# Branch B's query projected by features and read per group from scratch memory, in place of a token-major projection with transposes in attention

## The chip, the cores and the metric

The kernel runs on one NeuronCore of a Trainium2 chip. The metric is device time in microseconds (us) of one execution; the program is launched once and works through both layers. The engines are named as in the profile: PE (TensorE, with its weight loads as PEld), DVE (VectorE), ACT (ScalarE), POOL (GpSimd) and SP (SyncE, which here issues nearly all DMAs).

## The reference

Two layers of a hybrid decoder block over 512 tokens with 1024 features, all in float32. What matters here is branch B, a sliding-window attention with 16 query heads and 2 key/value heads of 64 features each:

```python
proj = h @ w_in                      # h = rmsnorm(x); all branches share one projection
# columns: DeltaNet q | k | v | z | beta | decay | SWA q (1024) | k (128) | v (128) | gates A, B
q = partial_rope(q_in.reshape(B, S, 16, 64), positions)   # rotates features 0..15 of each head
k = partial_rope(k_in.reshape(B, S, 2, 64), positions)
x1, x2 = xr[..., :8], xr[..., 8:]
rot = concatenate([x1 * cos - x2 * sin, x2 * cos + x1 * sin])
scores = einsum(q, k) * 64 ** -0.5   # 128 queries against the own and the previous 128 keys
p = softmax with a sink per head; o = p @ v
```

Branch A is a gated DeltaNet (short convolutions, decays, a chunked delta rule). Both branches are projected up, gated, merged, projected out, and followed by a feed-forward part with 4096 hidden features.

## The kernel before

**Numbers.** Every large product is made of three products in a reduced float32 type: each operand is split into a high part (a cast on ACT) and a remainder (a subtraction on DVE), and PE adds high x high, high x low and low x high in PSUM. Weights come as chunks of up to 128 x 1024 from one packed tensor; `load` (line 278) issues the DMA on SP, `prefetch` (376) makes the pair `wh`, `wl`. Six raw chunks (`WR`) and four pairs (`LOOK`) can be held ahead of use.

**Two ways to project.** `mm_a` (396) makes a feature-major tile: the weights stand still in PE and all 512 tokens move, 24 products of 512 columns to a PSUM tile of 128 features. `mm_a2` does it in two halves of 256 tokens. `mm_b` (415) and `mm_b4` (448) make token-major tiles: 128 tokens stand still and a strip of weight columns moves. Branch B's columns (beta, decay, q, k, v: 1296 in all) are projected token-major before, in three strips of `NB` = 432 columns, n = 0, 1, 2, each for four tiles of 128 tokens.

**Start of a layer.** The first strip is interleaved with the norm of the four token tiles. `turn` (542) transposes a normed tile on PE, `turned` (549) splits it into `hT`. In layer 0 this order is written out by hand for PE, ACT, DVE and SP (the `Order` object, 179, from line 610 to 677; `spin` fills PE with idle transposes). In layer 1 (681 to 691) only PE's order is written out, continuing that of the feed-forward tail. `rotary` (229) makes `cs`, the cosines and sines by token, once.

**Rest of B's projection.** Strips n = 1 and 2 (786) are projected into four PSUM tiles at a time, alternating between two sets (`four`, 492). `evac_b` (722) copies the strips into the token-major tiles `qt[t]` and `kv[t]`. In the middle of n = 1 stands `decays` (760): it cumulates DeltaNet's decays on PE, writes them to scratch memory, reads them back broadcast for each of 8 heads (`D`, 256 KB each), masks them on POOL, takes four exponentials a head on ACT (782) and writes them out again (`dd`).

**Attention beside other projections.** A loop over 16 groups (1044) runs one `att_group(t, g, e)` beside units of other projections: `MIX` lists them (G: merge gate B, K: DeltaNet key with convolution, A: gate A). A unit is one `mm_a`, 24 products of 512 columns, into the two-buffer PSUM pool `PM`. `att_rope(t)` (901) rotates all 16 query heads and 2 key heads on POOL, in tiles of 128 x 128. `att_prep` (918) splits v and transposes k. `att_q(t, g)` (941), called for every second group, transposes four 128 x 128 blocks of `qt[t]` on PE (945), scales, casts and splits them on ACT (950) and DVE (951) into the two tiles `qT` of 64 high rows and 64 low rows. `att_group` makes scores, masks, softmax on ACT and DVE, then transposes the probabilities (`ps_pt`, 1007) and multiplies them with v. The result replaces q in `qt[t]`.

**Order.** Outside the `Order` regions a planner places the instructions: it simulates the engines with costs of its own and picks, on each engine, the ready instruction that stands first in the program. On the chip each engine then runs its list strictly in that order. SP's list holds the weight loads and the scratch traffic together.

## Time and profile before

| | |
|---|---|
| median of 3 runs | 1817.72 us (1816.64 to 1817.88) |
| profiled execution, its own time | 1816.19 us |
| its span, first to last instruction | 1814.5 us |
| mean granted PE clock | 0.999 |
| busy: PE, DVE, ACT, POOL | 99%, 76%, 56%, 12% |
| HBM read, written | 239.38 MB, 37.36 MB |

PE's busy share includes modelled ends: a product is listed as busy until its result is drained, so consecutive products overlap in the list. What one product costs is the distance from its start to the next one's start. A row of the timeline gives start, duration, engine, line, operation, result and operands, and in brackets the engine's idle time ahead of it with what ended it.

### The profile page before, as it was taken

Reading aid. Unit: us, or ns where it says so; the run is one execution under the profiler, and the core shown is the slowest. Engines: PE = TensorE matmul, PEld = TensorE weight load, DVE = VectorE, ACT = ScalarE, POOL = GpSimd, SP = SyncE. Lnnn points to the kernel's source line nnn. Section 1 sums busy time; section 2 is a strip of 40 time slices with the busy share of each in tenths; the row PEclk is TensorE's granted clock in tenths of the full one; section 3 lists DMA queues with packets and bytes.
Section 4 is the critical chain, followed back from the end, with each engine's and each line's share of the span. In section 5 each row is a group of like instructions: output and inputs, shape, how many; then the busy total and the mean of one; then the engine's idle time right before and its main releaser. Section 6 shows DMA issues by size and latency. Waiting matters only on the chain.

```text
span 1814.5 us, 28394 instructions
## 1 busy us (share of the span) xinstructions
PE 1794.6 (99%) x10252; PEld 1524.7 (84%) x10252; DVE 1375.1 (76%) x2590; ACT 1007.5 (56%) x2065; POOL 210.6 (12%) x386
## 2 busy tenths in 40 slices
PE   9999999999999999999999999999999999999998
PEld 8878878888788888989898887888877888889896
DVE  5499796887666878898556997968875669698973
ACT  6678742444434656566556877234443347566572
POOL 0322102221101000000013221022111010000000
PEclk9999999999999999999999999999999999999999
DMA  5633447655463254554445334585545533555551
GB/s 201 203 112 121 111 146 226 178 172 152 117 208 129 82 164 156 174 180 145 168 160 176 106 127 111 169 232 159 163 140 154 171 116 105 174 162 164 174 178 56
DMA packets 146431, 278.60 MB, mean 154 GB/s; under 512 B 33569, under 2 KB 66657, under 8 KB 146290
## 3 DMA queue, kind: packets, MB, share of 16 engines
q1 hardware_dynamic: 145778, 276.75, 49.2%
q8 instruction: 81, 1.33, 0.3%
q14 instruction: 60, 0.49, 0.1%
q0 software_dynamic: 512, 0.03, 0.0%
HBM read 239.38 MB, written 37.36 MB: 153 GB/s over the span
## 4 chain that ended last, share of the span: by engine, by line
PE 88%; DVE 4%; ACT 4%; DMA 2%; issue 1%; POOL 0%; SPq 0%; DVEq 0%; POOLq 0%; ACTq 0%
PE ps_b L459 3%; PE ps_b L461 3%; PE ps_b L463 3%; PE ps_f L400 2%; PE ps_f L401 2%; PE ps_f L402 2%; PE ps_us L400 2%; PE ps_ud L400 2%; PE ps_us L401 2%; PE ps_ud L401 2%; PE ps_ud L402 2%; PE ps_us L402 2%; PE ps_vp L400 2%; PE ps_vp L402 2%; PE ps_vp L401 1%; PE ps_qp L401 1%
## 5 line engine op out<-in xcount | busy, mean ns | idle before, releaser
L384 ACT CAST wh<-wr 128x1024 fp32r<-128x1024 f32 (+2 forms) x368 | 372.7, 1019 | 430.4 <-PE ps_us L401 60.2
L385 DVE TENSOR_TENSOR wl<-wr,wh 128x1024 fp32r<-128x1024 f32 (+2 forms) x368 | 434.9, 1189 | 183.8 <-ACT wh L384 180.2
L526 POOL TENSOR_TENSOR pr<-pq,pw 128x1 f32<-128x1 f32 x16 | 9.8, 615 | 790.1 <-DVE pq L525 790.1
L459 PE MATMUL ps_b<-wh,h_h 128*128 128x432 f32 (+1 forms) x192 | 71.1, 370 | 0.0
L461 PE MATMUL ps_b<-wl,h_h 128*128 128x432 f32 (+1 forms) x192 | 70.4, 367 | 0.0
L463 PE MATMUL ps_b<-wh,h_l 128*128 128x432 f32 (+1 forms) x192 | 70.3, 366 | 0.0
L400 PE MATMUL ps_f<-g_h,wh 128*128 128x512 f32 x160 | 62.4, 390 | 0.0
L401 PE MATMUL ps_f<-g_l,wh 128*128 128x512 f32 x160 | 62.4, 390 | 0.0
L402 PE MATMUL ps_f<-g_h,wl 128*128 128x512 f32 x160 | 62.2, 389 | 0.0
L401 PE MATMUL ps_qp<-h_l,wh 128*128 128x512 f32 x128 | 53.9, 421 | 0.0
L400 PE MATMUL ps_vp<-h_h,wh 128*128 128x512 f32 x128 | 53.7, 420 | 0.0
L402 PE MATMUL ps_vp<-h_h,wl 128*128 128x512 f32 x128 | 53.7, 419 | 0.0
L995 ACT ACTIVATE M<-M,nm 128x128 f32<-128x128 f32 x128 | 49.8, 391 | 5.9 <-DVE nm L990 5.8
L400 PE MATMUL ps_qp<-h_h,wh 128*128 128x512 f32 x128 | 51.8, 405 | 0.0
L343 DVE TENSOR_TENSOR wr<-wr 128x512 f32<-128x512 f32 x72 | 47.5, 685 | 5.5 <-DMA wr<-in_weights_dram 5.2
L400 PE MATMUL ps_kp<-h_h,wh 128*128 128x512 f32 x128 | 51.6, 403 | 0.0
L402 PE MATMUL ps_qp<-h_h,wl 128*128 128x512 f32 x128 | 51.4, 401 | 0.0
L401 PE MATMUL ps_vp<-h_l,wh 128*128 128x512 f32 x128 | 51.3, 401 | 0.0
L401 PE MATMUL ps_ga<-h_l,wh 128*128 128x512 f32 x128 | 51.0, 398 | 0.0
L400 PE MATMUL ps_gb<-h_h,wh 128*128 128x512 f32 x128 | 51.0, 398 | 0.0
L402 PE MATMUL ps_kp<-h_h,wl 128*128 128x512 f32 x128 | 50.9, 398 | 0.0
L402 PE MATMUL ps_ga<-h_h,wl 128*128 128x512 f32 x128 | 50.7, 396 | 0.0
(435 smaller groups left out, 5928.4 us busy)
## 6 DMA issues: line engine op xcount, KB each, us to landing
wr<-in_weights_dram SPq DMA_DIRECT2D x320, 512.0 KB, 3.6
wr<-in_weights_dram SPq DMA_DIRECT2D x24, 432.0 KB, 5.2
D<-dd SPq DMA_DIRECT2D x32, 256.0 KB, 2.7
xd<-xo SPq DMA_DIRECT2D x12, 512.0 KB, 3.0
xt<-xd SPq DMA_DIRECT2D x24, 256.0 KB, 4.5
D<-gd SPq DMA_DIRECT2D x16, 256.0 KB, 6.2
dd<-D SPq DMA_DIRECT2D x16, 256.0 KB, 5.2
kkd<-kk SPq DMA_DIRECT2D x16, 256.0 KB, 2.0
```

The source lines that it names most:

```text
L343: tt(out=o_, in0=i0, in1=i1, op=ALU.add)
L384: nc.scalar.copy(wh[:, :w], wr[:, :w])
L385: sub(out=wl[:, :w], in0=wr[:, :w], in1=wh[:, :w].bitcast(F32), op=ALU.subtract)
L400: mm(ps, lhsT=wh[:, k, :], rhs=hi, start=k == 0, stop=False)
L401: mm(ps, lhsT=wh[:, k, :], rhs=lo, start=False, stop=False)
L402: mm(ps, lhsT=wl[:, k, :], rhs=hi, start=False, stop=k == KT - 1)
L459: mm(pss[t], lhsT=hi[:, tsl], rhs=wh[:, r, :], start=k == 0 and not onto, stop=False, skip_group_check=onto)
L461: mm(pss[t], lhsT=hi[:, tsl], rhs=wl[:, r, :], start=False, stop=False, skip_group_check=onto)
L463: mm(pss[t], lhsT=lo[:, tsl], rhs=wh[:, r, :], start=False, stop=k == KT - 1, skip_group_check=onto)
L526: ptt(out=r, in0=q1, in1=mhalf[:, 0:1], op=ALU.pow)
L995: act(out=M[:, j * P:(j + 1) * P], in_=M[:, j * P:(j + 1) * P], func=AF.Exp, bias=nm[:, j:j + 1], accum_out=den[:, j:j + 1])
```

## The change

Branch B's columns are split. Beta, decay, k and v (272 columns, `w_bkv`) stay token-major, now as the only strip; the weights come in three chunks with 2, 3 and 3 blocks of 128 rows (`BK`). q is projected feature-major in eight units like the other `mm_a` units. The host packs its columns so that feature d of all 16 heads lies together: unit u holds features 8u to 8u+7 of all heads, rows ordered (d, head). So units 0 and 1 hold the features that are rotated, and the rotation is six operations of DVE on whole 128 x 512 tiles, with cosines and sines turned to the same layout once (`turned_rotary`, layer 0; written to `csd` and read back in layer 1). Scaled high and low parts (`q_out`) are written to scratch memory `qd`; attention reads each group's `qT` from there by one DMA, issued one group ahead. `att_q`'s transposes, ACT and DVE work go, as do the copies into `qt` and the rotation of q on POOL. `decays` moves to the third q unit. In layer 1 the first q unit is put into the written-out order in two halves.

```diff
+    def turned_rotary(rot):
+        big = X4("cse")
+        b4 = big.rearrange("p (t s n) -> p t s n", t=NT, s=2)
+        for t in range(NT):
+            for s in range(2):
+                nc.gpsimd.tensor_copy(
+                    b4[:, t, s, :].rearrange("p (d h) -> p d h", d=HALF),
+                    cs[:, t, s, :].unsqueeze(2).broadcast_to([P, HALF, QH]))
+        for s in range(2):
+            ps = PS("ps_cs")
+            for t in range(NT):
+                tr(ps[:, t * P:(t + 1) * P], b4[:, t, s, :], ident)
+            nc.scalar.copy(rot[s], ps)
+            dma(csd[s], rot[s])
...
+    def mm_bkv(ps, ws, aT, t, ks=range(KT)):
+        tsl = slice(t * P, (t + 1) * P)
+        for k in ks:
+            hi, lo = aT[k]
+            j, = [i for i, (a, b) in enumerate(BK) if a <= k < b]
+            wh, wl = (w[:, k - BK[j][0], :] for w in ws[j])
+            mm(ps, lhsT=hi[:, tsl], rhs=wh, start=k == 0, stop=False)
+            mm(ps, lhsT=hi[:, tsl], rhs=wl, start=False, stop=False)
+            mm(ps, lhsT=lo[:, tsl], rhs=wh, start=False, stop=k == KT - 1)
...
-            for t in (None, 1, None, None, 2, None, 3):
+            for t in (None, 1, None, 2, None, 3):
...
-            for j in range(2):
-                part(0, j)
+            part(0, 0, 2)
             turned(ps0[1], 0, qs[1])
+            part(0, 2, 4)
             feed(2)
             q = sq(2)
             xs = [half(1, g) for g in range(2)]
-            part(0, 2)
+            part(0, 4, 5)
             ps1 = [turn(x_) for x_ in xs]
-            feed(3)
             rs.append(rstd("nr", *q))
-            part(0, 3)
+            part(0, 5, KT)
...
-            part(1, 0)
-            part(1, 1)
+            part(1, 0, 5)
             ps2 = [turn(x_) for x_ in xs]
             rs.append(rstd("nr", *q))
-            part(1, 2)
-            part(1, 3)
+            part(1, 5, KT)
...
-            part(0, 0, 6)
-            part(1, 0, 6)
-            part(0, 6, KT)
+            part(0, 0, 5)
+            part(1, 0, 5)
+            part(0, 5, KT)
+            part(1, 5, KT)
+            qf0 = PZ("ps_qf")
+            wq0 = weights()
+            mm_a2(qf0, hT, 0, wq0, range(0, 4))
             norm_turn(xs_next[2], 2, nxt[1])
-            part(1, 6, KT)
+            mm_a2(qf0, hT, 0, wq0, range(4, KT))
             norm_turn(xs_next[3], 3, nxt[1])
-            part(2, 0, KT)
-            part(3, 0, KT)
+            for a, b in ((0, 5), (5, KT)):
+                for t in (2, 3):
+                    part(t, a, b)
+            mm_a2(qf0, hT, 1, wq0)
...
         for t in range(NT):
-            evac_b(0, t, pb0[t])
+            nc.vector.tensor_copy(ba[:, t, :], pb0[t][:, 0:16])
+            nc.scalar.copy(kv[t][:, 0:256], pb0[t][:, 16:NB])
...
-        for n in range(1, 3):
-            pss = four(n)
-            mm_b4([p_[:, :NB] for p_ in pss], hT, decays if n == 1 else lambda: None)
-            for t in range(NT):
-                evac_b(n, t, pss[t])
+        rot = [T[2]("rot") for i in range(2)]
+        if l == 0:
+            turned_rotary(rot)
+        else:
+            for i in range(2):
+                dma(rot[i], csd[i])
+        qd8 = lambda i, u: qd[i, u * 8:(u + 1) * 8].rearrange("d h t -> (d h) t")
+
+        def q_out(u, src, scale=None):
+            hi, lo = pair(T[8], "qf")
+            if scale is None:
+                split(src, hi, lo)
+            else:
+                act(out=hi, in_=src, func=AF.Copy, scale=scale)
+                stt(out=lo, in0=src, scalar=scale, in1=hi.bitcast(F32), op0=ALU.mult,
+                    op1=ALU.subtract)
+            for i, a in enumerate((hi, lo)):
+                dma(qd8(i, u), a.bitcast(F32))
+
+        half_q = []
+        for u in range(NQU):
+            ps = qf0 if u == 0 else None
+            if ps is None:
+                ps = PM("ps_qf")
+                mm_a(ps, hT)
+            if u == 2:
+                decays()
+            if u >= 2:
+                q_out(u, ps, HD ** -0.5)
+                continue
+            a = T[1]("qa")
+            act(out=a, in_=ps, func=AF.Copy, scale=HD ** -0.5)
+            half_q.append(a)
+            if u == 1:
+                a, b = half_q
+                m = [T[3]("rm") for i in range(4)]
+                for i, (x_, r_) in enumerate(((a, 0), (b, 1), (b, 0), (a, 1))):
+                    tt(out=m[i], in0=x_, in1=rot[r_], op=ALU.mult)
+                tt(out=m[0], in0=m[0], in1=m[1], op=ALU.subtract)
+                q_out(0, m[0])
+                tt(out=m[2], in0=m[2], in1=m[3], op=ALU.add)
+                q_out(1, m[2])
...
-        def att_q(t, g):
-            ps = PS("ps_q")
-            for i in range(4):
-                j = g * 4 + i
-                tr(ps[:, i * P:(i + 1) * P], qt[t][:, j * P:(j + 1) * P], ident)
-            for e in range(2):
...
+        qgroups = qd[:, :, :, :].rearrange("a d (g j e) t -> (a d) g j e t", g=2, e=2)
+
+        def att_q(t, g, e):
+            a = T[7]("qT", F32R)
+            dma(c4(a.bitcast(F32)), qgroups[:, g, :, e, t * P:(t + 1) * P])
+            at["q", t, g, e] = a
...
+        att_q(*groups[0])
         for i in range(16):
+            if i < 15:
+                att_q(*groups[i + 1])
```

More of the change, by code (lines that the diff above doesn't have):

```diff
@@ L64, in chunk_order @@
         b_in = lambda w, r, c, n: out.append(("chunk", w, l, r, c, n))
-        for n in range(3):
-            for j in range(4):
-                b_in("w_in", j * 256, OFF_B + n * NB, NB)
+        for a, b in BK:
+            out.append(("chunk", "w_bkv", l, a * P, 0, (b - a) * NB))
+        for u in range(NQU):
+            a_in("w_q", u * 8)
         n_ = {"K": 0, "G": 0, "A": 0}
@@ L622, in hybrid_trunk @@
             sq = lambda t: (meansq(xts[t][:, :512], "nq0"), meansq(xts[t][:, 512:], "nq1"))
[L623 removed]
+            part = lambda t, a, b: mm_bkv(pb0[t][:, nbs], pre, hT, t, range(a, b))
             half = lambda t, g: norm_half(xts[t], gb, rs[t], g)
@@ L962, in att_group @@
                 att_rope(t + 1)
-            if e == 0:
-                att_q(t, g)
             w0 = max(t - 1, 0) * P
-            qh, den = at["q", e], sm.tile([P, 4], F32, name="den", bufs=4)
+            qh, den = at["q", t, g, e], sm.tile([P, 4], F32, name="den", bufs=4)
             kTh, kTl = kT[g]
```

86 lines of the change are left out of this document (43 added, 43 removed).

## The prediction

> **What bounds the kernel now.** I read the page first: shares of the engines and of the chain of waits.
>
> ```profile
> span 1814.5 us, 28394 instructions
> ...
> PE 1794.6 (99%) x10252; PEld 1524.7 (84%) x10252; DVE 1375.1 (76%) x2590; ACT 1007.5 (56%) x2065; POOL 210.6 (12%) x386
> ...
> PE 88%; DVE 4%; ACT 4%; DMA 2%; issue 1%; POOL 0%; SPq 0%; DVEq 0%; POOLq 0%; ACTq 0%
> ```
>
> PE sets the end nearly everywhere. So a step counts by the PE time it adds or removes, and by the PE waits it makes or ends. Second, the busy times by stage (span of the stage, then PE, PEld, DVE, ACT, POOL with counts, clock, DMA share, GB/s): layer 0's projection of B after its start, layer 0's attention, and the same two stages of layer 1.
>
> ```profile
> 33.00:71.00 38.00, 38.00 (x199) 36.61 (x198) 15.51 (x34) 27.43 (x69) 7.80 (x13) 1.00 0.75 243
> 71.00:245.00 174.00, 171.41 (x875) 138.97 (x874) 148.72 (x427) 131.86 (x386) 40.88 (x78) 1.00 0.37 113
> ...
> 930.00:968.00 38.00, 38.00 (x200) 36.65 (x199) 14.87 (x31) 25.95 (x66) 7.43 (x12) 1.00 0.75 241
> 968.00:1150.00 182.00, 178.61 (x907) 145.07 (x906) 154.89 (x441) 134.26 (x390) 44.16 (x80) 1.00 0.39 118
> ```
>
> In the projection stage PE has no gap, DVE is 40% busy and the DMA engines 75%. In attention PE idles 174 - 171.4 = 2.6 and 182 - 178.6 = 3.4 us, 6.0 in all, and DVE is 85% busy. These waits of PE, layer 0 then layer 1, say who is late there (times in total, count, longest):
>
> ```profile
> PE ps_pt L1007 <- ACT M L1001: 2.0, 3, 0.8
> ...
> PE ps_pt L1007 <- ACT M L1001: 1.9, 3, 0.7
> ```
>
> It is the softmax on ACT that PE's transposes of the probabilities wait for.
>
> **The change, part by part.** *The projection itself.* Third, the timeline of PE, for the distance of starts, 432 columns and 512 columns:
>
> ```profile
> 64.08 0.36 PE L459 MATMUL ps_b<-wh,h_h 128*128 128x432 f32 x1
> ...
> 64.66 0.36 PE L459 MATMUL ps_b<-wh,h_h 128*128 128x432 f32 x1
> ...
> 73.10 0.39 PE L400 MATMUL ps_gb<-h_h,wh 128*128 128x512 f32 x1
> ...
> 73.78 0.39 PE L400 MATMUL ps_gb<-h_h,wh 128*128 128x512 f32 x1
> ```
>
> Three steps lie between each two rows, so 0.193 us for 432 columns and 0.227 for 512: a fixed 0.013 plus 0.000417 a column, which gives 0.127 for 272 and 0.120 for 256. Before, a layer has 3 x 8 x 4 x 3 = 288 products of 432: 55.7 us. After, it has 96 of 272 (12.2) and 192 of 512 (43.5): 55.7 us. **0**. Splitting layer 1's first q unit in halves adds 24 products, 24 x 0.013 = **+0.3 us**.
>
> *The transposes in attention.* All 64 products of line 945, and one group of four with what follows it:
>
> ```profile
> L945 PE MATMUL ps_q<-ident,qt x64: 270/272/273, 76.6 to 1108.7; 128*128 128x128 f32 x64
> ...
> 76.61 0.60 PE L945 MATMUL ps_q<-ident,qt 128*128 128x128 f32 x4
> 76.97 0.47 PE L400 MATMUL ps_kp<-h_h,wh 128*128 128x512 f32 x1
> 77.28 0.39 PE L401 MATMUL ps_kp<-h_l,wh 128*128 128x512 f32 x1
> ```
>
> Four take 0.60 from first start to last end, so starts are (0.60 - 0.272) / 3 = 0.109 apart. The unit's product starts 0.36 after the first and takes 0.31 instead of 0.227 to the next: 0.36 + 0.08 = 0.44 for a group. There are 16 groups: **-7.0 us**, on the path, as PE's gaps there are 6.0 of 356 us. The turned cosines add 8 transposes in layer 0, 8 x 0.109 = **+0.9**.
>
> The Trainium skill ("TensorE: Matmul & The Clock Gate", Part 4, PE-mode transpose) gives about 275 ns for a transpose in a kernel's context; by it 56 fewer would be worth 15.4 us instead of 6.1. The row agrees as to duration, 272 ns, but the starts are 109 ns apart.
>
> *The start of layer 0.* Fewer columns per token tile leave PE less to do while the norms are made.
>
> ```profile
> 14.14 1.40 DVE L535 SCALAR_TENSOR_TENSOR xs<-x,nr,ps_row 128x512 f32<-128x512 f32 x2
> 15.37 1.04 PE L546 MATMUL ps_n<-ident,xs 128*128 128x128 f32 x8
> ...
> 16.62 1.29 DVE L552 TENSOR_TENSOR h_l<-ps_n,h_h 128x512 fp32r<-128x512 f32 x2
> ...
> 33.42 0.44 PE L459 MATMUL ps_b<-wh,h_h 128*128 128x432 f32 x1
> ```
>
> The second tile's transposes wait for its normed half; with a first weight chunk of 544 instead of 864 columns ahead of it I put them at 14.5 instead of 15.37. Behind them stand 81 products (10.3), three sets of eight transposes (2.4) and some 0.3 of waits: the stage ends near 27.5, 5.9 before 33.4. It hands 96 x 0.067 = 6.4 us of columns to the q units. Loss **+0.5**. A tile now costs PE 3.05 + 0.8 us against 1.29 + 1.40 on DVE plus ACT's cast, so DVE should keep up; ends: -0.5 (the smaller chunk lands sooner) and +2.0 (three tiles late by 0.5 each beside the 0.5).
>
> *What the q units add beside PE.* Per layer 8 casts and 2 copies on ACT replace 12 copies to `qt`, about even; DVE gets 8 splits and 6 rotation steps, 14 x 0.69 (the size of line 951, below) = 9.6 us in a stage where it idles 22. POOL makes 8 copies of 128 x 128:
>
> ```profile
> L912 POOL TENSOR_TENSOR rt<-qt,cs x8: 449/458/465, 69.3 to 1051.0; 128x128 f32<-128x128 f32 x8
> ...
> L951 DVE SCALAR_TENSOR_TENSOR qT<-ps_q,qT x32: 683/685/694, 79.0 to 1112.1; 64x512 fp32r<-64x512 f32 x32
> ...
> 32.87 0.32 ACT L256 ACTIVATE cs<-ang,hp 128x32 f32<-128x32 f32 x1
> ```
>
> 8 x 0.46 after 33.2 is 37, and rotation needs the tables at 27.5 + 0.9 + 2 x 5.44 = 39: hidden by the first two units, though by 2 us only. SP issues 16 writes and 16 reads more a layer, and two of the turned tables; weight loads stand behind the writes in its list, but run up to ten chunks (six raw, four split) ahead of use, 10 x 5.44 = 54 us: cost 0. The decays start at 27.5 + 0.9 + 16.3 = 44.7 in layer 0, and the first K unit, their first reader, ends at 27.5 + 0.9 + 43.5 + 10.9 = 82.8: cost 0. The writes are 4.2 MB in a stage that moves 243 GB/s at a share of 0.75: 13 us of full DMA time on 28.5, in 44 us. It fits, just; what is late first is the broadcast read of the decays.
>
> *The new wait there.* A q unit holds one of two PM buffers until ACT has cast it and DVE has split it, where four-tile sets had spare. And ACT has the decays. Layer 1, the decay product on PE and then ACT in order of time, with the copies of strip n = 1 among the exponentials:
>
> ```profile
> 940.34 0.30 PE L762 MATMUL ps_g<-lw,le 128*128 128x32 f32 x2
> ...
> 949.37 0.21 ACT L780 ACTIVATE egl<-D 128x4 f32<-128x4 f32 x1 [2.17 <-POOL D L778]
> ...
> 950.90 0.50 ACT L727 COPY qt<-ps_b 128x432 f32<-128x432 f32 x1
> ...
> 956.90 0.50 ACT L727 COPY qt<-ps_b 128x432 f32<-128x432 f32 x1
> ...
> 960.15 1.28 ACT L782 ACTIVATE D<-D,ngc 128x128 f32<-128x128 f32 x4
> ```
>
> From the decay product, exponentials fill ACT from +9.0 to +21.1, and copies got in at +10.6 and +16.6 only, because the decays stand first in the program. After, with zero at the end of unit u = 2, unit 4 ends at +10.9, its cast gets in at +16.6 and DVE frees the buffer at 16.6 + 0.6 + 0.7 + 0.1 = 18.0; PE has unit 5 until +16.3. Wait 1.6 a layer, **+3.2**. Ends: 0 (the cast gets in at once) and 22.5 - 16.3 = 6.2 a layer (it comes behind the last exponential), 12.4.
>
> *The trip through scratch memory.* The nearest row is the 256 KB round trip that the chain shows at the last head of DeltaNet, and PE's wait behind it:
>
> ```profile
> 462.10 3.77 DMA vxd<-kvx
> 466.02 3.40 DMA kvx<-vxd
> ...
> 469.95 0.49 PE L1264 MATMUL ps_y<-vs,Pt 128*128 128x128 f32 x2 [0.91 <-ACT vs L1247]
> ```
>
> From the end of unit 7 the first `qT` needs 0.6 + 0.7 + 7.2 = 8.5 us. PE has G and K units meanwhile, 2 x 5.44 = 10.9. If the planner puts the scores behind K, nothing is lost; right behind G, 3.1 a layer. I take 0.5, between no wait and the 0.9 of the row: **+1.0**, ends 0 and 6.2. Later groups are read a group ahead, over 8 us, and the DMA is at 0.37 there: 0. SP stands still while the first read waits for the last write; behind it are weights ten chunks ahead and K's scratch writes: 0.
>
> *What attention gets back.* ACT loses 2 x 0.59 and DVE 2 x 0.69 for each of 8 query blocks a layer, 9.4 and 11 us, and POOL's rotation goes. PE's 6.0 us of waits there are mostly behind ACT, so I take half, **-3.0**. Ends: -6.0 (all), and +2.0 (the order is planned anew, and one layer's waits for the softmax come twice).
>
> **Sum:** -7.0 + 0.9 + 0.3 + 0.5 + 3.2 + 1.0 - 3.0 = -4.1 us. The profiled execution, 1816.2 with a span of 1814.5, would take 1812.1; the median of the runs stands 1.5 higher, so I forecast 1817.7 - 4.1 = **1813.6 us**. All low ends give -12.3, all high ends +14.8.
>
> **Rivals.** *ACT holds the q units (slower).* The casts of units 4 and 5 come behind the last exponential in both layers, because D arrives later with the writes in the same DMA engines and ACT runs its list in order: +12.4 in place of +3.2, 1822.8. For it: ACT's solid 12 us, the DMA share of 0.75. Against: two copies did get in. It decides from a cast at +18.5 on: the wait is then 18.5 + 1.4 - 16.3 = 3.6 a layer, which with both layers eats the 4.1 saved; from +20.4 on the loss passes 0.2%.
>
> *Attention is filled by others (no change).* PE's order is planned around ACT and DVE; if the softmax stays as late as it is, half of the 7.0 turns into waits for it and none of the old waits goes: -4.1 + 3.5 + 3.0 = +2.4, 1820.1; with the casts in time as well, -0.8, 1816.9. For it: DVE at 85%; against: ACT and DVE lose more there than PE.
>
> *More than the sum.* No wait at the PM buffers or the first read and all 6.0 given back: -11.3, 1806.4. For it: attention's waits name ACT; against: the burst on ACT.
>
> *A transpose is worth its whole duration.* The 7.0 becomes 64 x 0.272 = 17.4 and the 0.9 becomes 2.2, so -4.1 - 10.4 + 1.3 = -13.2, 1804.5. For it: the mean duration in the row; against: the distances of starts, 0.109, which are what the next product waits for. The Trainium skill's price above ("TensorE: Matmul & The Clock Gate", Part 4) would come out here.
>
> **How the numbers follow.** About 0.2%, 3.6 us, is what a measurement of this kernel can tell from no change. Forecast 0.37, its own range 1809 to 1817; more than the sum 0.08; whole duration 0.02; attention filled 0.27; ACT holds 0.26. The forecast and the two larger gains make 0.47, of which the forecast's upper end passes 0.01 to no change: faster 0.46, same 0.27 + 0.01 = 0.28, slower 0.26. The range reaches from the larger gain to the slower rival: 1805.5 to 1824.
>
> **What would show it.** Line 945 gone, and products of 272 columns 0.127 apart (at 0.14, +1.2 a layer). The first product of the first q unit of layer 0 near 27.5. The gap ahead of q unit 6: 1.6, and 6 would be the slower rival. The first scores: no idle PE, or idle behind a DMA of `qd`. PE's wait for `M` halved in attention. If the projection stage has gaps at every unit, or weights are late, the sum is wrong in a part that I costed at nothing.

## The result, and the profile after

The changed kernel took 1826.87 us in the median of six runs (1825.28 to 1832.95), the kernel before 1817.8 in the same rounds. The ratio is 1.0057, with a 95% interval from 1.0043 to 1.0071: 0.57% slower, 9 us by the medians and 10 by the ratio, where the forecast was 4 us faster. It also lies above the range (1805.5 to 1824). The profiled execution took 1828.03 us, 1.2 above its median, as that of before lay 1.6 below its own; so the two traces differ by 11.85 us in span, 3 more than the medians.

The page of the changed kernel, its span, its busy times and its chain by engine:

```profile
span 1826.3 us, 28362 instructions
...
PE 1793.9 (98%) x10220; PEld 1508.5 (83%) x10220; DVE 1366.0 (75%) x2576; ACT 998.5 (55%) x2039; POOL 198.3 (11%) x346
...
PE 74%; DVE 7%; DMA 6%; ACT 6%; issue 4%; POOL 2%; SPq 1%; DVEq 0%; POOLq 0%; ACTq 0%
```

PE has 32 products fewer (64 transposes gone, 8 for the cosines and 24 halves added), as counted, and its busy time is lower. But PE held 88% of the chain before and holds 74% now: the time is not in products, it is in waits. PE's waits in the changed kernel (us in total, times, longest):

```profile
PE ps_y L1331 <- DVE rr L1328: 4.3, 6, 2.3
PE ps_s L1041 <- DMA qT<-qd: 2.8, 2, 1.9
PE ps_qf L435 <- DVE qf_l L838: 2.6, 2, 1.5
PE ps_pt L1071 <- ACT M L1065: 2.4, 3, 0.8
...
PE ps_o L1087 <- DVE pf_l L546: 2.0, 4, 1.5
PE ps_n L591 <- DVE xs L580: 1.7, 1, 1.7
PE ps_o L1087 <- POOL pc L1081: 1.6, 4, 0.6
```

In the kernel before, the wait for `rr` takes 1.2 us and the one for `pc` 0.6. The waits for `qT`, `qf_l`, `pf_l` and `xs` are not there, and the one for `M` is longer:

```profile
PE ps_pt L1007 <- ACT M L1001: 3.9, 6, 0.8
```

So PE waits 1.5 us less for the softmax (`M`), and 3.0 more for what is made of it, the split probabilities (`pf_l`) and the masked ones (`pc`). The timeline of PE in the changed kernel has, in layer 0 and in this order: the wait at the start, the first q unit, the wait ahead of q unit 6, the wait ahead of the first scores, and what follows them.

```profile
12.40 0.29 PE L458 MATMUL ps_b<-wh,h_l 128*128 128x272 f32 x1
14.40 1.38 PE L591 MATMUL ps_n<-ident,xs 128*128 128x128 f32 x8 [1.71 <-DVE xs L580]
...
26.80 0.29 PE L456 MATMUL ps_b<-wh,h_h 128*128 128x272 f32 x1
...
27.55 0.25 PE L743 MATMUL ps_cw<-ident,cwr 96*128 96x96 f32 x1
27.58 0.48 PE L435 MATMUL ps_qf<-h_h,wh 128*128 128x512 f32 x1
...
67.61 0.39 PE L437 MATMUL ps_qf<-h_h,wl 128*128 128x512 f32 x1
69.52 0.50 PE L435 MATMUL ps_qf<-h_h,wh 128*128 128x512 f32 x1 [1.53 <-DVE qf_l L838]
...
85.23 0.39 PE L437 MATMUL ps_kp<-h_h,wl 128*128 128x512 f32 x1
87.47 0.30 PE L1041 MATMUL ps_s<-kT_h,qT 128*128 128x128 f32 x1 [1.85 <-DMA qT<-qd]
...
89.38 0.42 PE L1041 MATMUL ps_s<-kT_h,qT 128*128 128x128 f32 x1
...
90.67 0.73 PE L435 MATMUL ps_kp<-h_h,wh 128*128 128x512 f32 x1
91.20 0.63 PE L436 MATMUL ps_kp<-h_l,wh 128*128 128x512 f32 x1
...
92.78 0.39 PE L437 MATMUL ps_kp<-h_h,wl 128*128 128x512 f32 x1
```

From 67.61 to 69.52 are 1.91 us where 0.227 is the distance of products: q unit 6 is 1.69 late. From 85.23 to 87.47 it is 2.01. And after that wait the products of 512 columns start 0.43 to 0.53 apart instead of 0.227. The windows of this stretch (length, PE, PEld, DVE, ACT and POOL busy, granted clock, DMA share, GB/s) show why:

```profile
84.00:88.00 4.00, 2.15 (x13) 1.56 (x12) 0.55 (x2) 0.26 (x1) 0.00 (x0) 1.00 1.02 275
88.00:90.00 2.00, 2.00 (x13) 1.87 (x13) 1.73 (x5) 0.85 (x1) 0.00 (x0) 0.80 0.60 220
90.00:92.00 2.00, 2.00 (x8) 1.77 (x8) 1.90 (x4) 1.98 (x11) 0.00 (x0) 0.50 1.01 317
```

The granted clock is 1.00 while PE idles, falls to 0.50 at 89.2, 1.7 us after the work has resumed, and is back at 1.00 from 92.6, 3.41 us later. From 89.38 to 92.78, six products of scores and five of 512 columns take 3.4 us in place of 6 x 0.111 + 5 x 0.227 = 1.8: the wait for q costs 1.6 us more than itself.

Where the 11.85 us lie, as distances between first starts in the two traces (first product of gate B, of the up-projection `ps_us`, of `ps_wo`, of layer 1's `ps_b`):

| stretch | before | after | difference |
|---|---|---|---|
| layer 0, start and B's projection | 71.04 | 75.11 | +4.07 |
| layer 0, attention | 175.26 | 177.27 | +2.01 |
| layer 0, from there to `ps_wo`, with the scan | 308.99 | 311.87 | +2.88 |
| layer 0, rest | 307.55 | 308.17 | +0.62 |
| layer 1, B's projection | 105.68 | 106.98 | +1.30 |
| layer 1, attention | 175.29 | 174.41 | -0.88 |
| layer 1, rest | 670.68 | 672.53 | +1.85 |

Attention, which was to give 10 us, gives nothing in the two layers together: 351.7 us here, 350.1 and 348.7 in two later runs with the same order of instructions, 350.6 and 350.3 in two profiles of the kernel before. The third row holds no edited line.

### The profile page after: what moved, and what is told of

Read it like the earlier page. It is cut to its first block, busy times and chain, and to the rows that moved or that the text cites. A ratio compares the mean times of both kernels' runs of the same rounds, so it can differ in the third digit from the quotient of the medians.

```text
span 1826.3 us, 28362 instructions
## 1 busy us (share of the span) xinstructions
PE 1793.9 (98%) x10220; PEld 1508.5 (83%) x10220; DVE 1366.0 (75%) x2576; ACT 998.5 (55%) x2039; POOL 198.3 (11%) x346
## 4 chain that ended last, share of the span: by engine, by line
PE 74%; DVE 7%; DMA 6%; ACT 6%; issue 4%; POOL 2%; SPq 1%; DVEq 0%; POOLq 0%; ACTq 0%
PE ps_f L435 2%; PE ps_f L436 2%; PE ps_f L437 2%; DMA fb<-fd 2%; PE ps_us L435 2%; PE ps_us L437 2%; PE ps_us L436 2%; PE ps_b L506 2%; PE ps_b L504 2%; PE ps_b L508 2%; PE ps_ud L436 2%; PE ps_ud L437 1%; PE ps_ud L435 1%; PE ps_qp L435 1%; PE ps_qp L436 1%
## 5 line engine op out<-in xcount | busy, mean ns | idle before, releaser
L436 PE MATMUL ps_kp<-h_l,wh 128*128 128x512 f32 x128 | 51.0, 399 | 0.0
L436 PE MATMUL ps_ud<-yT_l,wh 128*128 128x512 f32 x128 | 49.9, 390 | 0.8 <-DVE yT_l L546 0.8
L435 PE MATMUL ps_us<-oT_h,wh 128*128 128x512 f32 x128 | 50.0, 390 | 0.6 <-DVE qq L874 0.6
L435 PE MATMUL ps_ga<-h_h,wh 128*128 128x512 f32 x128 | 50.6, 395 | 0.0
L436 PE MATMUL ps_gb<-h_l,wh 128*128 128x512 f32 x128 | 50.5, 395 | 0.0
```

The costliest lines, as they stand in the source:

```text
L435: mm(ps, lhsT=wh[:, k, :], rhs=hi, start=k == 0, stop=False)
L436: mm(ps, lhsT=wh[:, k, :], rhs=lo, start=False, stop=False)
```

## The experiments

Each ratio is to the kernel before, in the same rounds.

**Attention alone, and the transposes put back.** The kernel before, with its own projection, but without transposes, splits and the 16-head rotation; q's own values are left out, `qT` comes from scratch memory filled once.

```diff
-            if e == 0:
-                att_q(t, g)              # 4 transposes, casts, splits
+            # all groups: qT by DMA from qd, one group ahead
+            dma(qrows[:, i * 2048:(i + 1) * 2048], a.bitcast(F32))   # qd filled once with hT
```

> The kernel before with the attention of the changed one alone: B's projection, its evacuations and q's strips stay; the 64 transposes, the splits behind them and the 16-head rotation are gone, and qT is read per group from scratch memory that was filled once, in layer 0, with the normalized activations' halves (4 transfers of 1 MB); q's own values are left out of the attention. The prediction's two gains (theory): 64 transposes at 0.109 us a start, 7.0 us, and 3.0 us that attention gets back: 1807.8 beside 1817.8. What the trace of the changed kernel shows behind its first scores (second theory): 0.66 us and 2.4 us shorter in the two layers, and 1.7 us more without the lowered clock: 4.8 us, so 1813.0. Filled by others (rival): the planner's products are spread over the same time and the waits for M and for the probabilities take the transposes' place: 1816 to 1818.

It took 0.9971 of the time before (0.9960 to 0.9983), 1813.31 us. That is 4 us gained by the medians and 5 by the ratio, about half of the 10. The second theory had the time, 1813.0, but from 0.7 and 2.4 us of attention and the clock; the stages give 1.8 and 1.9. Two of PE's waits have grown, from 3.9 us for `M` and 0.6 for `pc`:

```profile
PE ps_pt L1000 <- ACT M L994: 5.2, 6, 1.2
PE ps_o L1016 <- POOL pc L1010: 2.7, 4, 0.8
```

With the transposes gone PE idles for 9.1 us in the two attention stages where it idled for 6.3; nothing shows a gain from ACT's and DVE's lighter lists. To see which part gives the 4 us, the same kernel again with the 64 transposes put back into a buffer that nobody reads:

```diff
+            if e == 0:
+                ps = PS("ps_q")
+                for i in range(4):
+                    j = g * 4 + i
+                    tr(ps[:, i * P:(i + 1) * P], qt[t][:, j * P:(j + 1) * P], ident)
```

> The kernel before with the attention of the changed one, as before it (q read from scratch memory that was filled once; q's own values left out), but the 64 transposes of q are issued as in the kernel before, into a buffer that nobody reads; what stays away is their evacuation on ScalarE and VectorE and the rotation of 16 heads on GpSimd. Without them the kernel was at 0.9971 of the kernel before, 4.0 us less, and attention 1.8 us shorter in each layer. TensorE's count (theory): the 64 transposes start 0.091 us apart in the profile before, 5.8 us in all, and they come back in full where they are put back; the rest of attention gives 0 to 2 us: attention at 175 to 176 us again, the kernel at 1816 to 1819. Gaps (rival): the transposes lay in time in which PE waited for softmax anyway, and what was gained came from the evacuations: attention stays at 173.5 us and the kernel at 1813 to 1814.

It took 1.0014 (1.0006 to 1.0023), 1820.68 us: not the 0.9971 that the transposes in gaps would leave, but slower than before. The first products of gate B and of the up-projection bound the attention stage. Their groups (shortest, median and longest duration in ns, first and last start in us), layer 0 and layer 1, first of the kernel before:

```profile
L400 PE MATMUL ps_gb<-h_h,wh x64: 387/389/485, 71.0 to 218.8; 128*128 128x512 f32 x64
L400 PE MATMUL ps_us<-oT_h,wh x64: 389/389/468, 246.3 to 289.2; 128*128 128x512 f32 x64
...
L400 PE MATMUL ps_gb<-h_h,wh x64: 387/390/476, 968.5 to 1116.2; 128*128 128x512 f32 x64
L400 PE MATMUL ps_us<-oT_h,wh x64: 387/389/467, 1143.8 to 1186.8; 128*128 128x512 f32 x64
```

The same groups with the attention alone:

```profile
L401 PE MATMUL ps_gb<-h_h,wh x64: 387/390/481, 70.6 to 216.4; 128*128 128x512 f32 x64
L401 PE MATMUL ps_us<-oT_h,wh x64: 387/389/467, 244.1 to 287.1; 128*128 128x512 f32 x64
...
L401 PE MATMUL ps_gb<-h_h,wh x64: 387/389/480, 969.1 to 1114.9; 128*128 128x512 f32 x64
L401 PE MATMUL ps_us<-oT_h,wh x64: 389/389/472, 1142.5 to 1185.5; 128*128 128x512 f32 x64
```

And with the transposes put back:

```profile
L401 PE MATMUL ps_gb<-h_h,wh x64: 387/389/481, 70.4 to 219.3; 128*128 128x512 f32 x64
L401 PE MATMUL ps_us<-oT_h,wh x64: 389/389/470, 246.8 to 289.7; 128*128 128x512 f32 x64
...
L401 PE MATMUL ps_gb<-h_h,wh x64: 387/389/481, 969.4 to 1118.5; 128*128 128x512 f32 x64
L401 PE MATMUL ps_us<-oT_h,wh x64: 389/389/467, 1146.1 to 1189.1; 128*128 128x512 f32 x64
```

Attention takes 175.3 and 175.3 us before, 173.5 and 173.4 alone, 176.4 and 176.7 with the transposes. So putting 64 transposes back costs 2.9 + 3.3 = 6.2 us, 0.097 each (7 us by the medians of the whole kernel), and all else that attention is rid of (the evacuations and the rotation) is worth 1.1 + 1.4 = 2.5 us on the wrong side. PE idles for 7.7 us in these two stages, 1.4 more than before, so that much of the 2.5 is waiting. Freed time on ACT and DVE brought nothing here; the planner's new order is the likely reason of the 2.5, which no run shows.

**The projection alone.** The changed projection with its writes, and the attention of before on rows loaded from x in q's place.

```diff
+            dma(qt[t], x[t * P:(t + 1) * P, :])       # in place of q
-        att_q(*groups[0])                             # nothing read from qd
+            if e == 0:
+                att_q(t, g)                           # transposes as before
```

> The changed kernel's projection with the attention of the kernel before: q by features, rotated, split and written to scratch memory, but not read back; attention rotates 16 heads and transposes as before, on rows that are loaded from x in place of q (2 MB more to read in each layer). Additive (theory): what the projection adds in place by the trace, 4.1 us in layer 0 up to the first feature unit and 1.5 in layer 1, with nothing for the attention, 5.6 us over the kernel before: 1823.4. The prediction's own terms (0.3, 0.9, 0.5 and 3.2 us): 1822.7. The DeltaNet stages (rival): they are 2.9 and 1.4 us longer in the changed kernel with no edit in them; if the writes to scratch memory or the new buffers cause that, this kernel has it too, and comes to 1827; if it is not theirs, the stage from the first products of the scan to the up-projection takes what it takes in the kernel before, 188.6 us in layer 0.

1.0059 (1.0042 to 1.0076), 1827.8 us: 10 us, nearly twice the 5.6 of the theory. Its rival, which had the scan longer here too, had 1827. Attention takes 175.4 and 175.1 us in it, as before. In its trace the loss is 5.7 us by the first product of gate B in layer 0 (at 76.7), 5.6 in the scan of layer 0 and 4.9 in layer 1's projection, of which 2.0 are a wait of the transposes for a normed tile, with 3.41 us at half the clock behind it; the profiled execution, 1832.77 us, is 5 above the median, which is that much of this. The changed start is dearer than its first profile said: the first q unit, at 27.6 there, came at 27.5, 27.5, 29.3, 29.4, 29.7 and 30.0 in six other profiles with the same start. The granted clock parts them. In the last four it fell to 0.50 for 3.41 us at the wait for `xs` (1.72 to 1.81 us); in the other three (waits of 1.71, 1.26 and 1.08) it stayed at 1.00. From the transposes behind this wait to the first q unit are 14.4 to 14.7 us in the four and 13.1 to 13.2 in the three; the rest is that `xs` came 0.4 to 0.9 later. One window, first of the changed kernel's profile, then of a later run with the same order of instructions (the earlier evacuation, below) and a wait of 1.72:

```profile
16.00:18.00 2.00, 2.00 (x18) 2.00 (x17) 1.98 (x4) 2.00 (x6) 0.00 (x0) 1.00 0.90 291
...
16.00:18.00 2.00, 2.00 (x11) 2.00 (x10) 1.43 (x3) 1.57 (x5) 0.14 (x1) 0.50 0.94 371
```

**The q units: more buffers, or no burst ahead.** ACT's timeline of the changed kernel between units 2 and 7 (L837 is the cast of a unit, L820 the exponentials of the decays):

```profile
58.55 0.57 ACT L837 ACTIVATE qf_h<-ps_qf 128x512 fp32r<-128x512 f32 x1
59.02 2.44 ACT L820 ACTIVATE D<-D,ngc 128x128 f32<-128x128 f32 x8
...
62.44 3.61 ACT L820 ACTIVATE D<-D,ngc 128x128 f32<-128x128 f32 x12
...
68.17 0.57 ACT L837 ACTIVATE qf_h<-ps_qf 128x512 fp32r<-128x512 f32 x1
```

Between 59.1 and 68.2 no cast gets in, and unit 6 waits for the buffer. One variant gives it another buffer, one takes the burst away:

```diff
-                ps = PM("ps_qf")
+                ps = (PM, PM, PZ, PZ)[u % 4]("ps_qf")
```

> The changed kernel, but the q units go round four PSUM buffers (two of PM, two of PZ) where they had PM's two. The wait as a wait (theory): TensorE waits 1.69 us ahead of q unit 6 in layer 0 and 1.19 us in layer 1 only because both PM buffers are held until ScalarE's cast gets past the decay exponentials; with four buffers both go and the kernel is 2.9 us shorter than the changed kernel, 1824.0 beside 1826.9. The wait moves (rival): the casts still stand behind the exponentials, so the last units' halves are written as late as before, and the first read of q comes no earlier: the time lost ahead of unit 6 turns up ahead of the first scores (2.01 us there now, 3.7 or more then), and the kernel stays at 1826 to 1827.

```diff
             if u == 2:
-                decays()                    # all 8 heads' exponentials
+                dec = decays()              # yields behind each head
+                next(dec)
             if u >= 2:
                 q_out(u, ps, HD ** -0.5)
+                for _ in range((1, 2, 2, 2, 1, 0)[u - 2]):
+                    next(dec)
```

> The changed kernel, but the decay exponentials are not queued in one block behind q unit 2: one or two heads' stand behind each of units 2 to 6. Burst (theory): no cast of a q unit stands behind more than 3 us of exponentials, TensorE no longer waits ahead of unit 6 (1.1 to 1.7 us in layer 0 and 1.2 in layer 1 in the two profiles of this code), with two PM buffers as now, and the wait ahead of the first scores stays: 1824.0. Conserved (rival): as with four buffers, what is saved there is idle time ahead of the first scores, and the kernel stays at 1825.8 or above; a variant of the rival, exponentials now beside the last units' casts, would make that wait longer than 2.0 us.

With four buffers: 1.0041 (1.0026 to 1.0056), 1825.76 us, not told apart from the changed kernel. PE's rows of the first scores in it, layer 0 and layer 1:

```profile
86.57 0.30 PE L1041 MATMUL ps_s<-kT_h,qT 128*128 128x128 f32 x1 [2.84 <-DMA qT<-qd]
...
987.41 0.30 PE L1041 MATMUL ps_s<-kT_h,qT 128*128 128x128 f32 x1 [2.56 <-DMA qT<-qd]
```

The wait ahead of unit 6 is gone and the waits here have grown, 1.85 to 2.84 in layer 0. The buffers only passed the lateness on, as the rival had it. With the exponentials spread: 1.0012 (1.0002 to 1.0022), 1821.18 us, 6 us under the changed kernel by the medians and 8 by the ratios (4 by the ratio of the earlier evacuation, below, whose order of instructions is the changed kernel's), more than either theory gave: no wait ahead of any q unit (layer 1's projection 105.67 us, as before), idle 1.27 and 1.59 us ahead of the first scores, and no lowered clock anywhere in its profile. No other single edit gained as much. The two waits at the q units are 2.9 us of it; the first scores come no earlier than in the changed kernel (11.8 and 12.1 us behind gate B's first product), and what the rest is stays open.

**The first read.** One more unit ahead of the first scores, or the last unit's evacuation ahead of the next weights' cast:

```diff
-MIX = "G K K G K K G K K G K K G GA GA GA".split()
+MIX = "GK K G K K G K K G K K G GA GA G A".split()
```

> The changed kernel, but the first attention group has two feature units ahead of it (G and K) and every later unit goes one group earlier; the order of the units and their weights is the same, and the last group but one has one G less beside it. First read (theory): in layer 0 TensorE idles 2.01 us ahead of the first scores behind the transfer of qT from scratch memory and then runs 1.7 us late at a lowered granted clock, in layer 1 it idles 1.10; one more unit, 24 products of 0.227 us = 5.4 us, covers all of it, so the kernel is 4.8 us shorter than the changed kernel, 1822.1, with a granted clock of 1.00 throughout. Filler is only moved (rival): the unit now lacks at the end of the stage, where softmax sets the pace, and the wait comes back there as a wait of the transposes for M or of DeltaNet's first products; then 1826 to 1827 with no idle time ahead of the first scores.

```diff
-                mm_a(ps, hT)
+                mm_a(ps, hT, w=taken() if u == NQU - 1 else None)   # weights' next split behind q_out
```

> The changed kernel, but behind the last q unit its own evacuation (cast, subtraction, two writes) comes before the next weights' cast and subtraction, which stand ahead of it on ScalarE (1.05 us) and VectorE (1.23 us). Trip on the path (theory): the first scores follow B's end by the length of the trip through scratch memory; the low half is written about 1.5 us earlier, so the first scores come 10.9 us behind B's end where the changed kernel has 12.36, PE's idle time ahead of them falls from 2.0 to 0.5 us in layer 0 and from 1.1 to nothing in layer 1, and the kernel is 1.5 + 1.1 us shorter, and up to 1.7 more if the granted clock then stays at 1.00: 1822.6 to 1824.3. DMA queue (rival): the reads then meet the weights' transfers and land no earlier; 1826 to 1827, with 12 us or more from B's end to the first scores.

The shift took 1.0049 (1.0034 to 1.0064), 1827.03 us: PE no longer idles ahead of the first scores, and nothing is gained. PE's waits in its layer 0 attention, and then a window behind the last of them:

```profile
PE ps_pt L1071 <- ACT M L1065: 2.5, 2, 1.4
PE ps_o L1087 <- POOL pc L1081: 2.1, 1, 2.1
```

```profile
151.00:153.00 2.00, 2.00 (x12) 2.00 (x11) 1.71 (x6) 1.13 (x3) 0.00 (x0) 0.50 0.02 6
```

The products used early are missing later: PE waits for the softmax and the masked probabilities, and there too the clock is halved after 2.1 us of idling (in layer 1 the same wait of 2.1 is followed by 1.00). The rival was right.

The earlier evacuation took 1.0036 (1.0024 to 1.0047), 1824.03 us, just inside what the theory gave. But this edit did not change what ran: every engine and SP have the changed kernel's instructions in the changed kernel's order. ACT still casts the next weights ahead of the last unit, presumably since that cast is ready first, and DVE follows it:

```profile
76.59 1.05 ACT L419 CAST wh<-wr 128x1024 fp32r<-128x1024 f32 x1 [3.95 <-PE ps_qf L436]
77.54 0.59 ACT L837 ACTIVATE qf_h<-ps_qf 128x512 fp32r<-128x512 f32 x1
```

So this is the changed kernel once more, and the theory on these two lists stays untested. The first scores come 11.68 and 10.98 us behind gate B's first product where it was 12.36 and 11.44: that is the spread of executions. With 1.0057 and 1.0036 for one order of instructions, and 1.0047 for a twin of it further down, the change costs 0.4 to 0.6%.

**All mends.** Four buffers, exponentials spread, last unit first (which leaves the weights' cast ahead here too), and at the start the norm of the second tile ahead of the third weights' split on DVE; then also the first read cut in three, so that only 32 KB wait for the last write.

```diff
             part(0, 2, 4)
+            xs = [half(1, g) for g in range(2)]
             feed(2)
             q = sq(2)
-            xs = [half(1, g) for g in range(2)]
```

> All mends of the changed kernel at once: four PSUM buffers for the q units, exponentials spread, the last unit's evacuation ahead of the weights', and in the start of layer 0 the normalization of x1's halves ahead of the third weights' split on VectorE (x1's transposes wait 1.4 to 2.0 us for it now). Sum (theory): 1.2 at the start, 2.9 for the q units, 2.6 to 4.3 ahead of the first scores: 1826.9 - 6.7 to 8.4 = 1818.5 to 1820.2, about the kernel before (1817.4) and not clearly faster. Attention sets the pace (rival): the chain of the 16 softmax groups runs as long wherever it starts, and the earlier start is worth all of it: 1818; or (second rival) products that ran ahead of the first scores are missing later, and 1822 to 1824 is reached.

```diff
+            if (t, g, e) == (0, 0, 0):
+                for d0, d1 in ((0, HD - 8), (HD - 8, HD)):
+                    for i in range(2):
+                        rows = slice(i * HD + d0, i * HD + d1)
+                        dma(c4(a[rows].bitcast(F32)), qgroups[rows, g, :, e, t * P:(t + 1) * P])
```

> All mends, and the first group's read of q cut in three: the rows of units 0 to 6 are read before the last unit is written, the last unit's 8 features (2 transfers of 16 KB) behind it. Trip (theory): behind the last write only 32 KB are read where it was 256 KB beside three more reads of 256 KB, so PE's idle time ahead of the first scores (0.8 us in layer 0, 1.4 in layer 1 with all mends) goes, the first scores come 9.7 us behind B's end as in the kernel before, and the kernel is 2 us shorter than with the other mends alone: 1817.5, or 0.1% under the kernel before in the same rounds. Landing (rival): it is the landing of the last write and the fixed time of a transfer that count, not its size, or the planner's filler ahead of the scores; then 1819.5, and the idle time stays above half of what it was.

1.0005 (0.9996 to 1.0014), 1819.49 us, and 1.0002 (0.9993 to 1.0011), 1817.9 us: level with the kernel before. The start is mended (first q unit at 27.0 and 26.7). Cutting the read brings the first scores from 11.1 and 11.7 us to 10.7 and 11.2 behind gate B's first product, not to 9.7. PE idles 1.07 and 1.64 us ahead of them where it idled 0.61 and 1.20, as the planner now puts the scores four products earlier. The time is the theory's, the mechanism the rival's: the size of the read was a small part of the trip. Behind the 1.64 the clock fell to 0.50 again.

**The scan of layer 0.** It is not edited, yet it took 191.5 us from the first `ps_qk` to the first `ps_ud` where it took 188.6.

> The kernel before once more, for a second profile of it. Executions differ (theory): the stages from the scan to the up-projection, which no variant edits and which took 309.0 us in layer 0 and 310.8 in layer 1 in the first profile and 309.7 to 314.6 and 309.5 to 312.3 in five others, differ by 1 us or more from its own first profile. A lasting shift (rival): both stages are within 0.5 us of the first profile, so that the 1 to 3 us more in the other kernels are theirs.

The second profile of the kernel before (span 1816.6): 188.9 us, and from the up-projection to `ps_wo` 309.3 beside 309.0. In layer 1 the same stretch took 312.2 beside 310.8, so layer 1's part of the loss is the spread of executions and layer 0's is not. In all, the four profiles of kernels without q units have 188.6 to 189.4, the thirteen with them 189.9 to 194.2 (means 188.9 and 191.3). Layer 1's scan shows no such thing: 189.2 to 191.8 without and 188.3 to 192.4 with them. First suspect, the place of the scratch memory, with every engine's order unchanged:

```diff
-    csd = dr.tile([2, P, S], F32, name="csd")
-    qd = dr.tile([2, HD, QH, S], F32, name="qd")
     ...
     egd = dr.tile([32, P], F32, name="egd")
+    csd = ...; qd = ...                          # the same two, last
```

> The changed kernel with the same two declarations moved and nothing else: every engine's order of instructions is the changed kernel's. Addresses (theory): 2 us shorter than the changed kernel, 1824.5 to 1825, with PE's wait for the first head's gate in layer 0 (2.48 us) gone. Not addresses (rival): 1826 to 1827 and the wait there as long, 1 to 2.5 us.

> As the variant with the read cut in three, but the two new scratch areas (4.5 MB) are declared behind all others, so that the scan's own scratch lies where it does in the kernel before; every engine's order of instructions stays. Addresses (theory): the scan of layer 0, first products to up-projection, took 188.6, 188.9 and 189.4 us in three profiles of kernels without q's writes, and 189.9 to 194.2 in seven with them, 1 to 3 us of it in the first head's trips through scratch memory; if the place of that memory causes it, this stage is back at 189 and the kernel 2 us shorter than its twin. Not addresses (rival): the stage stays at 190 to 192, and both twins take the same time.

The first took 1.0047 (1.0034 to 1.0060), 1825.94 us, with a scan of 192.6; the second 1.0004 (0.9996 to 1.0013), 1819.11 us, with 191.3. Not the addresses. Second suspect, SP. Its timeline in the first head's gate, of the kernel before (start, duration of the issue):

```profile
343.59 1.79 SPq L1151 DMA_DIRECT2D vxd<-kvx  x4
345.48 0.39 SPq L1214 DMA_DIRECT2D ff<-sd  x1
```

And of the changed kernel:

```profile
349.69 2.86 SPq L1218 DMA_DIRECT2D vxd<-kvx  x4
352.64 0.40 SPq L1281 DMA_DIRECT2D ff<-sd  x1
```

Four issues take 1.07 us longer, one of them 1.41 us by itself, and `ff`, for which the gate waits, stands behind them. Four or eight transfers of 16 bytes more at the start of SP's list:

```diff
+        pad = s1("pad", 4 * 4)                       # 4, then 8
+        for i in range(4):
+            dma(pad[0:1, i * 4:(i + 1) * 4], x[i:i + 1, 0:4])
```

> The changed kernel with four transfers of 16 bytes more at the start of SP's list in layer 0, into a tile nobody reads; SP's list is otherwise the same, PE's order too. In two executions of the changed order of instructions 18 of some 25 slow DMA issues on SP (over 0.8 us where 0.32 to 0.45 is usual) fell on the same of its 900 transfers, one of them on the first write of vxd in the first head of layer 0's scan (1.41 and 1.38 us), ahead of the read of ff that its gate waits for; in the kernel before the slow issue falls on the read of egb (1.21 and 1.14), which nobody waits for. Place in SP's list (theory): with four more ahead of it the slow issue falls four transfers earlier, on the write of vxd no longer; sd to ff takes 2.6 us as in the kernel before where it took 3.7, the scan is 188.6 to 190 us instead of 191.5 and 192.6, and the kernel 1 to 3 us shorter than the changed one. Tied to the transfer (rival): the write of vxd is slow again and the scan stays at 190 to 192.

> As the variant with four small transfers more, but eight: by the theory the slow issue falls eight transfers earlier, on the read of kvx or the write ahead of it, and vxd's first write takes 0.3 to 0.5 us; by the rival it is slow again.

> All mends with the first read cut in three, and four small transfers of 16 bytes more at the start of SP's list. Theory: the scan of layer 0 goes from 190.6 to 188.6 to 189.5 us, the kernel to 1816 us, 0.1% under the kernel before; rival: as without them, 1817.9.

SP's timeline with four more:

```profile
347.12 2.93 SPq L1218 DMA_DIRECT2D vxd<-kvx  x4
```

The slow issue goes with the transfer, not with its place in the list, and with eight more it is there again (3.02 us for the four). 1.0043 (1.0027 to 1.0059), 1826.38 us; the single run with eight took 1830.18; the mended kernel with four more 0.9992 (0.9983 to 1.0001), 1817.06 us, scan 190.8. So this theory falls as well. What is shown is that layer 0's scan is longer in every profile with the q units than in any without, and that about 1 us of it is that issue in twelve of the thirteen; the variant with the projection alone lost 5.6 us there without it, and the attention alone had it (1.32 us) in a scan of 189.4. Why it is slow, and what the rest is, stays open.

## Why the prediction was wrong

Three steps failed. What attention gets back had the wrong sign, the trip through scratch memory was under-sized, and the clock and the scan were put at nothing. The terms in their order, for the sum in place of -4.1:

- *The projection itself, 0, and the halves, +0.3:* right. Six starts of 272 columns lie between 26.80 and 27.55, 0.125 each.
- *The 64 transposes, -7.0:* right in kind, and nearly in size: 6.2 by the stages. The distance of starts was the measure, not the duration of 0.272; the rival that counted whole durations is out. The Trainium skill's price of 275 ns ("TensorE: Matmul & The Clock Gate", Part 4, PE-mode transpose) is a duration; an estimate that takes it as a cost gives 64 x 0.275 = 17.6 us in this kernel, where putting the transposes back cost 6.2.
- *What attention gets back, -3.0:* the step that failed most, in sign. It read ACT's and DVE's relief as PE's gain. PE's idle time there rose from 6.3 us to 9.1 with the attention alone and to 7.7 with the transposes put back, which show +2.5. In the changed kernel the waits for `M` did fall, from 3.9 to 2.4, the sign that was to be looked for, but those for `pf_l` and `pc` rose by 3.0. The bound of +2.0 had named the reason, a new order, and was too small.
- *The start, +0.5:* right as far as it went. The first q unit was to come near 27.5 and came at 27.5, 27.5 and 27.6 where the clock stayed at 1.00. In four of seven profiles the clock fell at the wait for `xs`, and the mean is 28.7 against 27.0 for no loss: +1.7, within the end of +2.0, but mostly by the clock, which the term did not hold.
- *The cosines, +0.9:* 1.6 in this profile. Two products of 512 columns and the eight transposes take from 33.80 to 35.90, where the products alone take 0.45. Some 0.3 is a wait for POOL, and the first transposes start 0.24 apart instead of 0.109.
- *The new wait at the q units, +3.2:* the right mechanism and size as a wait, 1.69 + 1.19 = 2.9. The slower rival, 6 a layer, didn't come. But without the burst 4 to 8 us go, more than the wait.
- *The trip through scratch memory, +1.0:* under-sized. The first scores came 12.36 and 11.44 us behind gate B's first product; the estimate was 8.5. PE had 10.35 us of products meanwhile and lost 2.0 and 1.1 waiting, together +3.1, within the end of 6.2. In layer 0 the low half's write was issued 2.9 us behind that product (1.3 estimated), the read 4.0 later and the scores 5.5 behind the read (3.6 each). The estimate left out that weights' cast (1.05 us on ACT) and split (1.23 on DVE) stand ahead of the last unit's, and that other transfers fill the same DMA engines (a share of 1.02 in the window of 84 to 88). Which of these counts how much, no run shows.
- *Nothing for the clock:* 1.6 us behind the first scores in this profile, in no term and in no bound.
- *Nothing for the scan:* +2.4 in the means, outside all edited code, cause open.

The sum is -6.2 + 2.5 + 0.3 + 1.7 + 1.6 + 2.9 + 3.1 + 1.6 + 2.4 = +9.9. Measured are 9 by the medians and 10.4 by the ratio, with an interval of 7.8 to 12.9, and 6.5 by the ratio of the earlier evacuation, which ran the same order once more. The attention stages of the trace hold +1.1, and four of these terms make +1.0. The prediction's high ends add up to +16.8, not to +14.8; its range doesn't hang on that sum. Of the rivals, the slower one (1822.8) was nearest in time, but by another mechanism than it named. That attention is filled by others (1820.1) named what happened there: it had 3.5 us of new waits, and the attention alone shows 2.8. The mended kernel takes away the q units' waits, the start's and a part of the others; the clock falls in one of four profiles of it and there once. It ends level with the kernel before; no version here beats it clearly.

## What to carry to other kernels

A transpose that PE doesn't wait for costs about its distance of starts, not its duration; taking it out gains less where PE then waits for others sooner. Relief on another engine need not come back at all, least of all where a planner lays out a new order. Where a planner decides the order, look in the trace whether an edit changed it before its time is read as the edit's. Work that goes through memory adds a trip whose every step queues behind others (the casts on ACT, the splits on DVE, the transfers on the DMA engines): cost it from the last producer's place in each of these lists, which here is read from the trace and not shown by a run. Where one buffer's wait is caused by a burst on another engine, spread the burst; more buffers handed the lateness on.

## What the runs showed that was not expected

PE's granted clock fell to half eleven times in seven of the 17 profiles, each time for 3.41 us and at a wait of PE of 1.64 to 2.26 us (the program's first wait and its end left out): five times at the start, three times at the first scores, once each in attention, in layer 1's start and in the scan. At fifteen other waits of 1.64 to 2.84 it stayed at 1.00. One kernel has both: the shift waits 2.11 us in each layer's attention, and the clock fell in layer 0 alone. With four buffers, behind the wait of 2.84:

```profile
89.00:91.00 2.00, 2.00 (x12) 1.65 (x11) 1.86 (x5) 1.98 (x11) 0.00 (x0) 1.00 0.99 328
```

So the length of the wait alone doesn't decide, and executions of one order differ by 1.6 us at the first scores and 1.2 to 1.6 at the start for such a fall. The Trainium skill ("TensorE: Matmul & The Clock Gate", Part 1) has the clock follow PE's activity in a window that runs by itself, which fits waits of equal length with different ends; its advice to leave no gap above some 3 us ("Why this matters for your kernels") is not enough here, as gaps of 1.64 to 2.26 us were followed by half the clock.

SP's slow issues are partly fixed to the program: in the changed kernel and its twin with the same order, 25 and 26 of 900 transfers took over 0.8 us to issue, and 18 of them are the same. A third profile of that order, of the earlier evacuation, has 23, of which 13 and 16 are among these.
